# Padding three small SBUF tiles of a four-layer decoder trunk so that the large tiles start on multiples of 128 bytes

## The chip, the cores and the metric

The kernel runs on one core of one Trainium2 chip. Its metric is the device time of one execution in microseconds. Three runs of the kernel before took 856.57, 856.60 and 856.96 us, a median of 856.6. The profile is of one more execution of the same program.

## The reference

The reference passes 256 tokens of 1024 float32 features through four pre-norm residual layers, in the order A, B, C, A. Cut to what matters:

```
for i in range(4):                                  # kinds A, B, C, A
    h = rms_norm(x, norm_gain[i])
    y = mixer[i % 3](h, weights of the layer)
    x = x + y

A: u, v, z = h @ w_in            (1024 -> 3 x 2048); v = rms_norm(v)
   mixed = tril(w_s[g]) @ v + b_s            per 128-token chunk, 8 groups of 256 columns
   y = (u * mixed * silu(z)) @ w_out         (2048 -> 1024)
B: 3 groups of q, k, v with 8 heads of 128, and a gate z: h @ w_in  (1024 -> 10240)
   q, k: rms_norm with gains, rotary on the first 32 of 128 dims
   masked softmax attention per group, the groups joined by their softmax denominators
   y = (o * silu(z)) @ w_out                 (1024 -> 1024)
C: xc, z = h @ w_in              (1024 -> 2 x 2048)
   pooled = causal means of xc over windows 2, 4, 8, 16, minus xc
   y = ((pooled @ w_grp) * scale * silu(z)) @ w_out      (2048 -> 1024)
```

## The kernel before, in words

Everything is computed in float32 accuracy by products of two parts. Each operand is split into a high part (`hi_of`, L81, a ScalarE copy into the type fp32r) and a low part (`lo_of`, L84, a VectorE subtraction), and each product is three TensorE instructions that add up in PSUM: high x high, high x low, low x high (`mm3`, L75, its three lines L77 to L79). In every row of the trace the name behind `<-` stands first for the moving operand, which streams through the array column by column, and second for the stationary one, of which 128 columns are loaded before.

All projection weights come as one stream of 272 units of 512 KB. `load_units` (L127) starts their DMAs on SP's queue into 4 buffers `wr`, `split_units` makes `w…h` and `w…l` in 7 buffers each, and `next_unit` (L156) hands them out in order. A unit holds two K tiles (128 features each) of 512 columns.

The normed, transposed activations h^T lie in two tiles, `hTh` and `hTl` (L187), 8 K tiles of 256 tokens. There are three ways to use them:

- `proj_tok` (L251): 512 columns of w move, 128 tokens of h^T are stationary. Layer A has 12 such calls (v, z, u), layer B 16 (q/k and two groups' values), layer C one.
- `proj_feat` (L275): 256 tokens of h^T move, 128 columns of w are stationary. Layer B has 2 such calls (gates), layer C 7; `group` (L797) does the same with the pooled tiles `cd`, 4 times with half the K tiles.
- the third group's values in layer B (`v2p`): 256 columns of w move, h^T is stationary, 4 times.

`proj_out` (L289) multiplies each layer's y by the output weights: 512 columns of w move, the stationary operand is `y` in layers A (tag `v`), `yb` in B and `cy` in C. The last steps of it prepare the next layer's h^T. Transposes go through TensorE with the identity `ident` moving.

The other work (norms, activations, rotary, softmax, pooling) is written as generators that are resumed between pieces of the weight stream (`spawn`, `tick`, L93 to L107). Every engine keeps the order of the program as it is written out (L909 to L918).

Tiles are laid out in SBUF in the order in which their pools first meet them: first the pool `cp` (constants, x, h^T, small statistics), then `wp` (weights), then the pool of the layer. The size of each tile of a partition is rounded up to a multiple of 32 bytes, so one small tile moves the start of all that come behind it. These are the small tiles in question:

```
184  m05 = cp.tile([P, 4], F32, tag="m05", name="m05")        # exponents for the power -0.5
340  bsT = cp.tile([P, 8], F32, tag="bs", name=f"bs{layer}")   # layer A, bias of the groups
729  csc = pl.tile([P, 16], F32, name="csc")                   # layer C, scale of the channels
```

Of the kernel before, what the change touches and what calls it, by code (L numbers as in the profile page):

```python
# [48 lines left out]
def hybrid_trunk_kernel(ctx, tc, x, wts, norm_gainT, a_v_gain, a_wsT, a_bsT, b_gl, b_gv, c_scaleT,  # L49
# [7 lines left out]

    # ---------------------------------------------------------------- helpers
    def pp(name):
# [15 lines left out]
    def mm3(out_ap, lh, rh, start, stop):  # L75
        """out += l.T @ r with l and r given as (hi, lo) pairs."""
        nc.tensor.matmul(out_ap, lh[0], rh[0], start=start, stop=False, skip_group_check=True)  # L77
        nc.tensor.matmul(out_ap, lh[0], rh[1], start=False, stop=False, skip_group_check=True)  # L78
        nc.tensor.matmul(out_ap, lh[1], rh[0], start=False, stop=stop, skip_group_check=True)  # L79
# [6 lines left out]

    # ------------------------------------------------------------- interleaving
    # Work beside the stream of weight products: generators that are resumed
    # between pieces of the stream, `yield n` pieces later.
    tasks = []  # L90
# [21 lines left out]
    def need(key):  # L112
        """Go on with the tasks until one has finished `key`."""
        n = 0
        while key not in done:
            tick()
            n += 1
            assert n < 1000, (key, sorted(map(str, done)), [(e[1].__name__, e[1].gi_frame.f_lineno) for e in tasks])

    # --------------------------------------------------------- weight stream  # L120
    raws = []
# [15 lines left out]
    def split_hi(n):  # L137
        """The high parts of the first n units of the stream."""
        while split[0] < min(n, n_units):
            u = split[0]  # L140
            load_units(u + 1)
            hi, lo = pair(wp, [P, 2, HALF], "w", f"w{u}", W_BUFS)
            hi_of(hi, raws[u])
            units.append((hi, lo))
            split[0] += 1

    def split_units(n):
        """Both parts of the first n units of the stream."""
        split_hi(n)
        while lowered[0] < min(n, n_units):  # L150
            u = lowered[0]
            lo_of(units[u][1], raws[u], units[u][0])
            lowered[0] += 1
            load_units(u + 1 + RAW_BUFS)

    def next_unit():  # L156
        """The next two K tiles of 512 columns of the weight stream."""
        u = used[0]
        used[0] += 1
        split_units(u + 1)  # L160
        return units[u]

    def step(i, ahead=AHEAD):
        """After piece i of a unit: the tasks that are due, then the splitting of the weights ahead."""
        tick()
        if i % 2 == 0:
            split_hi(used[0] + ahead)
        else:
            split_units(used[0] + ahead)

    # ------------------------------------------------------------ start
    xt = [cp.tile([P, D], F32, tag=f"x{t}", name=f"x{t}") for t in range(2)]
# [10 lines left out]
    make_identity(nc, ident)  # L183
    m05 = cp.tile([P, 4], F32, tag="m05", name="m05")
    nc.gpsimd.memset(m05, -0.5)
    junk = cp.tile([P, HALF], BF16, tag="junk", name="junk")
    hTh = cp.tile([P, KT, S], F32R, tag="hTh", name="hTh")  # L187
    hTl = cp.tile([P, KT, S], F32R, tag="hTl", name="hTl")
    # the tensor engine's clock rises while it is busy
    warm = atp("warm")  # L190
# [4 lines left out]

    # ------------------------------------------------------------- norm, h^T
    def half_ss(t, n, ss):
# [16 lines left out]
    def norm_transpose(layer, t, xs):  # L214
        """h^T of a token tile: resumed between the high parts and around the low parts of the K tiles."""
        pts = []
        for n in range(2):
            pt = (trp if n else atp)(f"hp{layer}{t}{n}").rearrange("p (k c) -> p k c", c=P)
            for k in range(4):
                nc.tensor.transpose(pt[:, k], xs[:, n, k * P:(k + 1) * P], ident)  # L220
            pts.append(pt)
        sl = slice(t * P, (t + 1) * P)
        for k in range(KT):
            nc.scalar.activation(hTh[:, k, sl], pts[k // 4][:, k % 4], AF.Copy, scale=gT[:, layer, k:k + 1])  # L224
            yield k
        for k in range(KT):
            nc.vector.scalar_tensor_tensor(hTl[:, k, sl], pts[k // 4][:, k % 4], gT[:, layer, k:k + 1],  # L227
                                           hTh[:, k, sl].bitcast(F32), op0=ALU.mult, op1=ALU.subtract)
            yield KT + k
# [19 lines left out]

    # ------------------------------------------------------------ projections  # L250
    def proj_tok(name, skew=None):  # L251
        """512 columns of h @ w, token-major: two PSUM tiles. With skew the first token tile goes ahead."""
        o = [pp(f"{name}_{t}") for t in range(2)]
        if skew is not None:
            ws = [next_unit() for j in range(4)]
            for t in range(2):
                need(("h", skew, t))
                for k in range(KT):
                    w = ws[k // 2]
                    mm3(o[t], h_t(k, t), (w[0][:, k % 2], w[1][:, k % 2]), k == 0, k == KT - 1)  # L260
                    if k % 2:
                        tick()
                        if t == 1:
                            split_units(used[0] + min(k // 2 + 1, W_BUFS - 4))
            return o
        for j in range(4):
            w = next_unit()
            for kk in range(2):
                k = 2 * j + kk
                for t in range(2):  # L270
                    mm3(o[t], h_t(k, t), (w[0][:, kk], w[1][:, kk]), k == 0, k == KT - 1)
                step(kk)
        return o

    def proj_feat(name):  # L275
        """512 columns of (h @ w)^T: two PSUM tiles of two 128-feature tiles."""
        o = [pp(f"{name}_{i}") for i in range(2)]
# [11 lines left out]
    def proj_out(layer, nkt, yT):  # L289
        """x += y @ w_out, then the norm of the next layer; yT(kt, t) gives the (hi, lo) stationaries."""  # L290
        acc = [[pp(f"wo{layer}_{t}{n}") for n in range(2)] for t in range(2)]
# [41 lines left out]

    # ---------------------------------------------------------------- layer A
    def load_a(layer, j):
# [3 lines left out]
        nc.gpsimd.dma_start(wsT, a_wsT[j])  # L339
        bsT = cp.tile([P, 8], F32, tag="bs", name=f"bs{layer}")  # L340
        nc.gpsimd.dma_start(bsT, a_bsT[:, j])
        # keep j <= i (row j, columns i)
        for g in range(8):
# [4 lines left out]
    def layer_a(layer, consts, pl, mid):  # L348
# [9 lines left out]
        def v_task(n, o):  # L358
# [13 lines left out]
            if n < 3:  # L372
                return
            # rows of w_s^T scaled by the tokens' rms of v
            yield 1
# [82 lines left out]

    # ---------------------------------------------------------------- layer B
    def load_b():  # L460
# [20 lines left out]
    def layer_b(layer, consts, pl):  # L481
# [6 lines left out]
        def qk_task(hp, g, o):  # L488
# [20 lines left out]
            def rotate(t):  # L509
                """Gains and rotary on the first 32 dims."""  # L510
                ra = pl.tile([P, 4, ROPE], F32, tag="ra", name=f"ra{hp}{g}{t}", bufs=1)
# [88 lines left out]

        # (head, group, key tile) pieces of p^T; the two query tiles side by side for key tile 0
        chunks = (((0, 0, 0), (0, 1, 0)), ((0, 2, 0), (0, 0, 1), (0, 1, 1)), ((0, 2, 1), (1, 0, 0), (1, 0, 1)),
# [3 lines left out]
        def mix_task(hp, vals, szT):  # L606
# [42 lines left out]
            def gated(h):  # L649
                """(o * silu(z))^T of a head."""  # L650
                sl = slice(h * S, (h + 1) * S)
                nc.vector.tensor_tensor(szT[:, sl], o[:, sl], szT[:, sl], op=ALU.mult)
                hi_of(yh[:, h], szT[:, sl])
                yield 1
                lo_of(yl[:, h], szT[:, sl], yh[:, h])
# [34 lines left out]
        def gate(b):  # L690
            """silu(z)^T of four heads."""
            zp = proj_feat(f"bz{b}")
# [33 lines left out]

    # ---------------------------------------------------------------- layer C
    def layer_c(layer, pl):
        csc = pl.tile([P, 16], F32, name="csc")
        nc.gpsimd.dma_start(csc, c_scaleT)  # L730
# [122 lines left out]

    # ------------------------------------------------------------------ layers
    sss = [tiny(2, f"ss_{t}") for t in range(2)]
# [52 lines left out]

    # every engine keeps the order of this program  # L909
    last = {}  # L910
# [9 lines left out]

# [1 line left out]
def _units(w):  # L922
    """[K, 512] columns as [K / 256, 128, 2 * 512] units."""
    k = w.shape[0] // 256
# [120 lines left out]
```

## Time and profile before

| | |
|---|---|
| median of three runs | 856.6 us |
| profiled execution, span | 854.8 us |
| TensorE busy | 844.9 us (99%), 4600 products |
| VectorE busy | 547.4 us (64%) |
| ScalarE busy | 489.2 us (57%) |
| GpSimd busy | 55.9 us (7%) |
| weight loads on SP's queue | 272 of 512 KB, 3.9 us from issue to landing |
| mean DMA rate | 175 GB/s |

The span runs from the first to the last instruction of the profiled execution; the run's time is 1.8 us longer in the median. Products of TensorE are pipelined: a 512-column product is shown with about 0.39 us from its start to its end, but the next one starts before that end. What counts for the time is therefore the step from the start of one product to the start of the next, which is read from the first column of the timeline.

### The profile page before, as it was taken

The page shows a single profiled execution, that of the slowest core. Times are in us where ns is not written, and L with a number is a line of the kernel's source. Part 1 is how long each engine was busy: PE and PEld are TensorE (multiplying, and loading weights), DVE is VectorE, ACT ScalarE, POOL GpSimd, SP SyncE. Part 2 cuts the span into 40 slices and gives each one's busy share as a digit, 9 for nine tenths or more (in the row PEclk, how much of TensorE's full clock was granted, in tenths as well). Part 3 has the DMA queues.
Part 4 walks back from the last instruction along what each step waited for, and adds up shares of the span by engine and source line. Part 5 has one row for each costly group of instructions (what it writes and reads, how often), then busy time and mean ns, then how long its engine had stood idle before and what let it go on. Part 6 is the DMA issues. An engine that isn't in the chain of part 4 may idle for free.

```text
span 854.8 us, 12424 instructions
## 1 busy us (share of the span) xinstructions
PE 844.9 (99%) x4600; PEld 721.5 (84%) x4600; DVE 547.4 (64%) x932; ACT 489.2 (57%) x918; POOL 55.9 (7%) x79
## 2 busy tenths in 40 slices
PE   8999999999999999999999999999999999999998
PEld 6888888888988888888888889999988888888886
DVE  6766556546746667667667575797754776555551
ACT  7665444336668677677677566455443666434340
POOL 1201000000001021021021012000000000000000
PEclk9999999999999999999999999999999999999999
DMA  8756554552754345345345267447564466454541
GB/s 279 281 204 214 196 189 149 187 194 89 243 177 154 121 148 174 122 149 175 122 148 173 74 222 265 158 147 246 197 207 148 140 228 205 158 176 169 166 154 50
DMA packets 41500, 149.57 MB, mean 175 GB/s; under 512 B 4864, under 2 KB 4880, under 8 KB 41184
## 3 DMA queue, kind: packets, MB, share of 16 engines
q1 hardware_dynamic: 40320, 144.72, 50.7%
q0 software_dynamic: 976, 4.05, 1.5%
q8 instruction: 36, 0.59, 0.3%
q14 instruction: 24, 0.20, 0.1%
q10 hardware_dynamic: 144, 0.02, 0.0%
HBM read 147.72 MB, written 1.05 MB: 174 GB/s over the span
## 4 chain that ended last, share of the span: by engine, by line
PE 86%; ACT 7%; issue 2%; DVE 2%; POOL 2%; DMA 1%; SPq 0%; POOLq 0%; DVEq 0%; ACTq 0%
PE wo L77 6%; PE wo L79 6%; PE wo L78 6%; PE qk L77 4%; PE qk L78 4%; PE qk L79 4%; PE z L77 4%; PE u L77 3%; PE u L78 3%; PE u L79 3%; PE z L79 3%; PE z L78 3%; PE v L78 3%; PE v L79 3%; PE v L77 3%; ACT junk L498 2%
## 5 line engine op out<-in xcount | busy, mean ns | idle before, releaser
L503 POOL TENSOR_TENSOR qr<-qm,m 128x4 f32<-128x4 f32 x24 | 30.3, 1271 | 226.1 <-DVE qm L502 226.1
L507 ACT ACTIVATE qn<-qk,qr 128x128 f32<-128x128 f32 x96 | 27.5, 381 | 15.1 <-POOL qr L503 15.1
L498 ACT ACTIVATE junk<-qk 128x128 bf16<-128x128 f32 x96 | 26.8, 279 | 7.5 <-PE qk L79 4.9
L421 DVE TENSOR_TENSOR sz<-u,sz 128x512 f32<-128x512 f32 x16 | 11.0, 686 | 29.1 <-PE u L79 29.1
L224 ACT ACTIVATE hTh<-hp,gT 128x128 fp32r<-128x128 f32 x64 | 17.5, 382 | 16.6 <-PE hp L220 16.6
L205 POOL TENSOR_TENSOR r<-ms,m 128x1 f32<-128x1 f32 x8 | 5.4, 669 | 289.3 <-DVE ms L203 289.3
L319 DVE TENSOR_TENSOR x<-wo,x 128x512 f32<-128x512 f32 x16 | 11.0, 689 | 20.1 <-PE wo L79 20.1
L227 DVE SCALAR_TENSOR_TENSOR hTl<-hp,gT,hTh 128x128 fp32r<-128x128 f32 x64 | 18.0, 343 | 8.2 <-ACT hTh L224 8.1
L363 ACT ACTIVATE junk<-v 128x512 bf16<-128x512 f32 x16 | 9.6, 600 | 18.9 <-PE v L79 18.7
L364 DVE TENSOR_TENSOR vv<-v,kc 128x512 f32<-128x512 f32 x16 | 10.9, 688 | 13.7 <-ACT junk L363 12.8
L498 ACT ACTIVATION_READ_ACCUMULATOR junk<-qk 128x1 f32 x96 | 19.0, 198 | 0.0
L447 ACT ACTIVATE sz<-z 128x512 f32<-128x512 f32 x16 | 9.5, 598 | 16.3 <-PE z L79 15.6
L516 DVE TENSOR_TENSOR ra<-qn,kcb 128x64 f32<-128x64 f32 x48 | 10.6, 221 | 12.0 <-ACT qn L507 10.9
L528 PE MATMUL qt<-ident,qn 128*128 128x128 f32 x96 | 14.6, 274 | 2.2 <-DVE qk22l L536 0.4
L198 ACT ACTIVATE junk<-x 128x512 bf16<-128x512 f32 x16 | 10.2, 639 | 11.1 <-DVE x L319 9.5
L528 PEld LDWEIGHTS qt<-ident,qn 128*128 128x128 f32 x96 | 11.4, 141 | 6.1 <-issue 2.0
L424 DVE SCALAR_TENSOR_TENSOR yy<-mx,bs,sz 128x256 f32<-128x256 f32 x32 | 14.0, 479 | 0.6
L598 ACT ACTIVATE p<-p,rl 128x384 f32<-128x384 f32 (+1 forms) x16 | 11.5, 768 | 4.6 <-DVE rl L597 4.6
L520 DVE TENSOR_TENSOR rb<-qn,kcb 128x32 f32<-128x32 f32 x96 | 13.7, 183 | 0.0
L594 ACT ACTIVATE p<-p,nb 128x768 f32<-128x768 f32 x8 | 7.5, 938 | 8.0 <-DVE nb L593 7.9
L502 DVE TENSOR_SCALAR qm<-qs 128x4 f32<-128x4 f32 x24 | 3.3, 164 | 13.0 <-ACT junk L498 13.0
L774 ACT ACTIVATE xc<-cx 128x512 f32<-128x512 f32 x8 | 4.7, 596 | 9.7 <-PE cx L79 9.4
(2770 smaller groups left out, 3273.1 us busy)
## 6 DMA issues: line engine op xcount, KB each, us to landing
wr<-in_wts_dram SPq DMA_DIRECT2D x272, 512.0 KB, 3.9
kc<-in_a_v_gain_dram POOLq DMA_DIRECT2D x2, 1024.0 KB, 6.8
x<-in_x_dram SPq DMA_DIRECT2D x4, 256.0 KB, 4.9
kc<-in_a_wsT_dram POOLq DMA_DIRECT2D x2, 512.0 KB, 8.9
out_dram<-x SPq DMA_DIRECT2D x4, 256.0 KB, 2.0
kcb<-in_masks_dram POOLq DMA_DIRECT2D x1, 576.0 KB, 8.5
kcb<-in_b_gl_dram POOLq DMA_DIRECT2D x1, 192.0 KB, 5.9
kcb<-in_rope_dram POOLq DMA_DIRECT2D x1, 64.0 KB, 8.4
```

The lines of the kernel that those rows point to most:

```text
L77: nc.tensor.matmul(out_ap, lh[0], rh[0], start=start, stop=False, skip_group_check=True)
L78: nc.tensor.matmul(out_ap, lh[0], rh[1], start=False, stop=False, skip_group_check=True)
L79: nc.tensor.matmul(out_ap, lh[1], rh[0], start=False, stop=stop, skip_group_check=True)
L224: nc.scalar.activation(hTh[:, k, sl], pts[k // 4][:, k % 4], AF.Copy, scale=gT[:, layer, k:k + 1])
L227: nc.vector.scalar_tensor_tensor(hTl[:, k, sl], pts[k // 4][:, k % 4], gT[:, layer, k:k + 1], hTh[:, k, sl].bitcast(F32), op0=ALU.mult, op ...
L424: nc.vector.scalar_tensor_tensor(y[:, sl], mxs[n][t][:, sl], bsT[:, 2 * n + gg:2 * n + gg + 1], us[t][:, sl], op0=ALU.add, op1=ALU.mult)
L498: nc.scalar.activation(junk[:, :HD], ov[t][:, h], AF.Square, accum_out=ssq[t][:, h:h + 1])
L503: nc.gpsimd.tensor_tensor(rq[t], ms, m05, op=ALU.pow)
L507: nc.scalar.activation(qn[t][:, h], ov[t][:, h], AF.Copy, scale=rq[t][:, h:h + 1])
L520: nc.vector.tensor_tensor(rb[:, hs, s0:s0 + 16], qn[t][:, hs, s1:s1 + 16], c, op=ALU.mult)
L528: nc.tensor.transpose(pts[t][:, h], qn[t][:, h], ident)
L598: nc.scalar.activation(f, f, AF.Copy, scale=rl[i][:, 0:1])
```

## The change

The three small tiles are made larger. The parts of them that are used stay as they were: 4, 8 and 16 columns.

```
-    m05 = cp.tile([P, 4], F32, tag="m05", name="m05")
-    nc.gpsimd.memset(m05, -0.5)
+    m05_row = cp.tile([P, 32], F32, tag="m05", name="m05")
+    nc.gpsimd.memset(m05_row, -0.5)
+    m05 = m05_row[:, :4]
...
-        bsT = cp.tile([P, 8], F32, tag="bs", name=f"bs{layer}")
+        bsT = cp.tile([P, 24], F32, tag="bs", name=f"bs{layer}")[:, :8]
...
-        csc = pl.tile([P, 16], F32, name="csc")
+        csc = pl.tile([P, 32], F32, name="csc")[:, :16]
```

The rest of the diff takes out comments; the line numbers behind L185 grow by one. The order of instructions on every engine and all operands' shapes are the same in both programs; the memset has 32 columns instead of 4.

What is different is where tiles start. In both programs the address of each tile within a partition is fixed when the program is built. This table has them for the tiles that matter, as the remainder by 512 bytes. The parts of them that the products use lie at multiples of 512 bytes from the tile's start.

| tile | start mod 512, before | after |
|---|---|---|
| `x`, `ident` | 128 | 128 |
| `hTh`, `hTl` (h^T) | 160 | 256 |
| `xs` (scaled x), `kc` (constants) | 288 | 384 |
| `wr`, `w…h`, `w…l` (weights) | 96 | 256 |
| layers A and B: `v`, `y`, `wsr`, `qk`, `pT`, `yb`, `sz`, `vv` | 96 | 256 |
| layer C: `cy` | 32 | 256 |
| layer C: `cd` | 416 | 128 |

Before, all of these but `x` and `ident` start 32 bytes past a multiple of 64; after, all of them start on a multiple of 128. The statistics of a few columns stay on multiples of 32 bytes in both.

## Rows read from the trace of the kernel before

**Rows 1.** The page, part 1 (busy us, share, count) and part 4 (the chain of waits).
```profile
PE 844.9 (99%) x4600; PEld 721.5 (84%) x4600; DVE 547.4 (64%) x932; ACT 489.2 (57%) x918; POOL 55.9 (7%) x79
...
PE 86%; ACT 7%; issue 2%; DVE 2%; POOL 2%; DMA 1%; SPq 0%; POOLq 0%; DVEq 0%; ACTq 0%
```

**Rows 2.** Windows, products with the tile hTh: us, PE busy (count), granted clock, DMA share, GB/s.
```profile
0.00:854.80 854.80, 544.51 (x2016) 1.00 0.53 175
```

**Rows 3.** Timeline of TensorE, layer A, h^T stationary: start us, duration us, line, out<-moving,stationary.
```profile
699.76 0.39 PE L77 MATMUL v<-w221h,hTh 128*128 128x512 f32 x1
...
705.36 0.39 PE L77 MATMUL v<-w223h,hTh 128*128 128x512 f32 x1
```

**Rows 4.** Timeline of TensorE, output product of the first layer A.
```profile
182.71 0.39 PE L79 MATMUL wo<-w57h,y02l 128*128 128x512 f32 x1
...
188.15 0.39 PE L79 MATMUL wo<-w59h,y02l 128*128 128x512 f32 x1
```

**Rows 5.** Timeline of TensorE, output product of layer C.
```profile
639.62 0.39 PE L77 MATMUL wo<-w200h,cy1h 128*128 128x512 f32 x1
...
645.11 0.39 PE L77 MATMUL wo<-w202h,cy1h 128*128 128x512 f32 x1
```

**Rows 6.** Timeline of TensorE, layer C, h^T moving.
```profile
539.78 0.28 PE L79 MATMUL cx<-hTh,w164l 128*128 128x256 f32 x1
...
542.61 0.28 PE L79 MATMUL cx<-hTh,w165l 128*128 128x256 f32 x1
```

**Rows 7.** Timeline of TensorE, third group's values, two of four runs (22 steps each).
```profile
273.05 0.28 PE L78 MATMUL v2p<-w88l,hTh 128*128 128x256 f32 x1
...
275.64 0.28 PE L79 MATMUL v2p<-w89h,hTl 128*128 128x256 f32 x1
...
337.27 0.28 PE L78 MATMUL v2p<-w106l,hTh 128*128 128x256 f32 x1
...
339.77 0.28 PE L79 MATMUL v2p<-w107h,hTl 128*128 128x256 f32 x1
```

**Rows 8.** Timeline of TensorE, scores of one head (8 steps).
```profile
283.03 0.28 PE L77 MATMUL s<-qk00h 128*128 128x256 f32 x1
...
283.99 0.28 PE L79 MATMUL s<-qk02h,qk02l 128*128 128x256 f32 x1
```

**Rows 9.** The chain of waits in order of time: eight transposes of h^T.
```profile
198.07 0.87 PE hp L220 x8
```

**Rows 10.** Groups by line, GpSimd: two memsets (busy us, mean ns).
```profile
L773 POOL MEMSET xc<- 128x32 f32 x8 | 0.8, 135 | 44.7 <-DVE cdd L791 44.7
...
L185 POOL MEMSET m<- 128x4 f32 x1 | 0.1, 101 | 0.0
```

**Rows 11.** The chain of waits in order of time, the start: its one DMA.
```profile
3.61 7.41 DMA wr<-in_wts_dram
```

**Rows 12.** Groups by line, VectorE and ScalarE, on tiles at either kind of start.
```profile
L319 DVE TENSOR_TENSOR x<-wo,x 128x512 f32<-128x512 f32 x16 | 11.0, 689 | 20.1 <-PE wo L79 20.1
L421 DVE TENSOR_TENSOR sz<-u,sz 128x512 f32<-128x512 f32 x16 | 11.0, 686 | 29.1 <-PE u L79 29.1
...
L198 ACT ACTIVATE junk<-x 128x512 bf16<-128x512 f32 x16 | 10.2, 639 | 11.1 <-DVE x L319 9.5 <-DMA x<-in_x_dram 1.4
...
L82 ACT ACTIVATE v02h<-vv 128x512 fp32r<-128x512 f32 x2 | 1.3, 633 | 0.1
```

**Rows 13.** The chain of waits in layer B, first and last piece of one stretch off TensorE.
```profile
308.96 0.72 ACT qk10h L530 x2
...
335.67 0.88 DVE qk12l L536 x2
336.68 0.63 PE qt L528 x4
```

**Rows 14.** Windows, layer C: us, busy us of PE, PEld, DVE, ACT, POOL, clock, DMA, GB/s.
```profile
555.60:577.00 21.40, 21.40 (x185) 21.40 (x183) 20.31 (x36) 11.59 (x16) 0.25 (x2) 1.00 0.44 147
```

## The prediction

> **What bounds the kernel now.** I read the page's first and fourth parts before anything else [rows 1]. TensorE is busy for 844.9 of 854.8 us and its products are 86% of the chain of waits, so the end is set by how closely TensorE's products follow one another. The granted clock is 1.00, the upper of its two levels (2.4 GHz), over the whole span [rows 2], where 512 columns at one a cycle would take 213.3 ns and 256 columns 106.7 ns. The next view was the timeline of TensorE, for the step from one start to the next inside long runs without a wait; each pair of rows there stands 24 products apart unless I say otherwise.
>
> - 512 columns of w moving, h^T stationary: (705.36 − 699.76) / 24 = 233.3 ns [rows 3].
> - the same 512 columns of w, layer A's y stationary: 5.44 / 24 = 226.7 ns [rows 4]; layer C's y stationary: 5.49 / 24 = 228.8 ns [rows 5].
> - 256 columns of h^T moving, w stationary: 2.83 / 24 = 117.9 ns [rows 6].
> - 256 columns of w moving, h^T stationary (the third group's values): 117.7 ns in one run and 113.6 ns in another, each over 22 steps [rows 7].
> - 256 columns in the scores, both operands from the q/k tiles: 0.96 / 8 = 120.0 ns [rows 8].
> - transposes, 128 columns, limited by loading 128 stationary columns: 0.87 / 8 = 109 ns [rows 9].
>
> The reader is to see two things. First, one and the same instruction (128x512, same moving tiles) has three paces, and only the stationary tile differs, that is, where it lies. Second, the paces lie above what either stream needs alone. From the scores to layer A's output product the moving operand grows by 256 columns and the step by 106.7 ns, exactly one column a cycle: streaming alone is at full rate although its tile lies 32 bytes past a multiple of 64. Loading alone is not held up either: 109 ns is 128 columns at half the array's rate, 106.7 ns, and 2 more. The excess belongs to the stretch of each product in which the next stationary columns are read beside the moving ones. Counted so, the floor is 109 ns for 256 columns and 109 + 106.7 = 215.7 ns for 512.
>
> **The change part by part.** No instruction is added, removed or moved on any engine; SP's, ACT's and POOL's queues issue the same DMAs in the same order. One memset grows from 4 to 32 columns, from 101 ns towards the 135 ns of the 32-column memsets of layer C [rows 10], and it lies inside the 7.41 us in which the chain waits for the first weights [rows 11]: 0, and 0.03 us without that cover. The 8- and 16-column DMAs carry the same bytes. All that is left is addresses: every operand of TensorE starts on a multiple of 128 bytes instead of 32 past a multiple of 64, and the distances between moving and stationary starts change for some pairs.
>
> VectorE and ScalarE: the trace holds both kinds of tile already. x lies on a multiple of 128, sz and vv lie 32 past a multiple of 64. VectorE's sum into x takes 689 ns, its product into sz 686; ScalarE reads x in 639 ns and vv in 633 [rows 12]. Cost and gain 0, with 3 to 6 ns an instruction as the bound either way, which hides beside TensorE.
>
> Weight DMAs: they land 3.9 us after issue, against a unit that lasts 12 x 233.3 ns = 2.8 us with four loads in flight; the chain has a DMA only at the start [rows 11]. I take 0, and keep 1 us either way for the 7.41.
>
> TensorE: no row shows an aligned operand inside a dense pair of streams, so I bound it. From below: every product falls to its floor. h^T stationary: layers A have 12 products x 8 K tiles x 2 token tiles x 3 = 576 each, B 16 x 48 = 768, C 48, together 1968, each 17.6 ns better: 34.6 us. Output products: 384 in the A layers and 96 in B at 11.0 ns, 5.3 us (B's taken at A's pace); 192 in C at 13.1, 2.5 us. 256 columns with w stationary: 9 x 96 with h^T and 4 x 48 in the pooled groups (taken at the same pace), 1056 at 8.9, 9.4 us. Third group's values: 192, one run of four at 117.7 and three at 113.6, mean 114.6, 5.6 each, 1.1 us. Scores: 72 at 11, 0.8 us. (The counts are from the code; rows 2 have 2016 products with the high part of h^T, two thirds of 1968 + 864 + 192.) Sum 53.7 us. From above: each form takes its worst row, +7 us (the slower rival). Between ends so far apart I take the lower one. The excess exists only where the two streams overlap, it changes with where a tile lies, and at present every start lies in the middle of a 64-byte stretch, so that if reads go in pieces of 64 or 128 bytes nearly every piece takes in two of them. That pieces have this size is my assumption; no row shows it.
>
> What comes back of the 53.7: layer B has four stretches in which the chain runs over ScalarE, VectorE and GpSimd from the q/k products to the transposes, the second from 308.96 to 336.68 us [rows 13]; three of 27.7 us and a first one of 15.1 us make 98 us, 11.5% of the span, and a faster TensorE only waits there: 6.2 us. In layer C VectorE is busy for 20.31 of 21.40 us [rows 14]; 7.5% less is 19.8 us: 0.5 us. So 53.7 − 6.7 = 47.0, the span goes from 854.8 to 807.8, and with the 1.8 us by which the median of 856.6 stands above the profiled span, 810 us.
>
> The Trainium skill (SBUF — State Buffer, Door 1, the note on cachelines) has 16-byte lines and a penalty for each crossing into a new line. Every start was a multiple of 32 already and stays one, so by that rule the step stays 233.3 ns and the sum is 0: it is the second rival's rule. The skill (TensorE: Matmul & The Clock Gate, Step-by-step) also says that loading the next weights takes no read bandwidth from the running product; by it 512 columns would have one pace whatever lies stationary, and 233.3 against 226.7 ns [rows 3, 4] disagree.
>
> **The rivals.**
>
> Only the distance counts. Layer A's y starts at the same phase of 512 bytes as w (both 96) and runs at 226.7; h^T is 64 bytes off and runs at 233.3; layer C's y is 64 off the other way. Afterwards all but the pooled tiles are at distance 0. Then h^T goes to 226.7: 1968 x 6.6 = 13.0 us; C's output 192 x 2.1 = 0.4; against it the 256-column products go to the scores' 120.0, also distance 0: 864 x 2.1 = 1.8 and 192 x 5.4 = 1.0. Net 10.6, less 11.5%: 9.4 us, 847 us. For it: it explains the order of the 512-column paces. Against it: 64 off is the slowest pace at 512 columns and the fastest at 256, and rows 7 show two paces at one distance.
>
> Nothing changes: pieces of 32 bytes or less, or an excess that belongs to this data type, or padding that does not reach the operands. 856.6 us. For it: streaming and loading alone are at full rate without alignment. Against it: the three paces of one instruction.
>
> Slower: one common phase is the bad one. With every tile on a multiple of 128, the moving stream, the stationary load and the other engines' accesses start in the same place of every 128 bytes and meet there. The price is that each form goes to its worst row: A's and B's output products from 226.7 to 233.3, 480 x 6.6 = 3.2 us; C's, 192 x 4.5 = 0.9; 256 columns to 120.0, 1056 x 2.1 = 2.2 and 192 x 5.4 = 1.0. Sum 7.3, so 864 us. It decides as soon as h^T's products do not fall below 233 ns. For it: the scores, both operands at one phase, are the slowest 256-column form. Against it: the output products at one phase are the fastest 512-column form.
>
> **How the numbers follow.** Aligned pairs read freely: 0.45, 810 us, its own range 802 (nothing comes back) to 833 (half the excess stays). Distance only: 0.22, 847. Nothing: 0.14. Slower: 0.17, around 864. Something between: 0.02, a small gain. Faster by over 0.2% (1.7 us, what a measurement of this kernel can tell) is 0.45 + 0.22 + 0.02 = 0.69, within it 0.14, slower 0.17. The range goes from 800 to 861: it leaves out most of the slower case and a remainder below.
>
> **What would show it.** In the changed profile the steps of the six forms above are read again. Right: 512 columns near 216 ns whatever is stationary, 256 columns near 109, VectorE's and ScalarE's means unchanged, TensorE's waits in layer B's four stretches longer. 226.7 and 120 ns everywhere speak for the distance alone, 233.3 and 117.9 unchanged for no effect, 233 beside 120 for the slower case. The forecast is wrong if h^T's step stays above 230 ns.

## The result and the profile after

The changed kernel takes 850.8 us in the median of four runs (850.58 to 850.96); the kernel before took 856.8 beside it (856.57 to 857.22). The ratio is 0.9931, with a 95% interval of 0.9919 to 0.9942: 6.0 us faster, where 47 were forecast. The profiled execution has a span of 849.1 us (before 854.8), so the two traces account for 5.7 of it.

With the runs for the experiments the kernel before shows that it has two times of its own: of all 45 runs of it, on several chips, 18 took 852.4 to 853.4 us and 27 took 856.2 to 857.3. All four that stand beside the change took the upper one, so the 6.0 us are against that; against the lower one the change is worth some 2 us. What the two times come from is followed up below.

The page's parts 1 and 4 of the kernel after answer to [rows 1]:

```profile
PE 837.2 (99%) x4600; PEld 724.6 (85%) x4600; DVE 546.8 (64%) x932; ACT 488.9 (58%) x918; POOL 57.4 (7%) x79
...
PE 86%; ACT 7%; DVE 2%; issue 2%; POOL 2%; DMA 1%; SPq 0%; POOLq 0%; DVEq 0%
```

Nothing has changed places: TensorE still sets the end. The products with `hTh`, over the whole span (us, PE busy, PEld, DVE, ACT, each with its count, then clock, DMA share, GB/s), as in [rows 2]:

```profile
0.00:849.10 849.10, 540.85 (x2016) 351.55 (x2016) 17.94 (x64) 17.49 (x64) 1.00 0.53 176
```

The granted clock is 1.00 again, so every difference in a step is one of cycles. The timeline of TensorE after (start us, duration us, line, out<-moving,stationary), two products that lie 24 steps apart for each form: h^T stationary as in [rows 3], layer A's y as in [rows 4], layer C's `cy` as in [rows 5], h^T moving as in [rows 6].

```profile
698.98 0.39 PE L77 MATMUL v<-w222h,hTh 128*128 128x512 f32 x1
...
704.42 0.39 PE L77 MATMUL z<-w224h,hTh 128*128 128x512 f32 x1
...
177.75 0.39 PE L79 MATMUL wo<-w57h,y02l 128*128 128x512 f32 x1
...
183.19 0.39 PE L79 MATMUL wo<-w59h,y02l 128*128 128x512 f32 x1
...
640.05 0.39 PE L77 MATMUL wo<-w201h,cy1h 128*128 128x512 f32 x1
...
645.49 0.39 PE L77 MATMUL wo<-w203h,cy1h 128*128 128x512 f32 x1
...
535.91 0.28 PE L77 MATMUL cx<-hTh,w164h 128*128 128x256 f32 x1
...
538.79 0.28 PE L77 MATMUL cx<-hTh,w165h 128*128 128x256 f32 x1
```

The first three pairs are 5.44 us apart, 226.7 ns a product: the 512-column forms have one pace now. h^T fell from 233.3, `cy` from 228.8, and y, which had 226.7 before, stayed. The last pair is 2.88 us apart: 120.0 ns, where it was 117.9. The third group's values, 22 steps apart as in [rows 7]:

```profile
333.70 0.28 PE L78 MATMUL v2p<-w106l,hTh 128*128 128x256 f32 x1
...
336.34 0.28 PE L79 MATMUL v2p<-w107h,hTl 128*128 128x256 f32 x1
```

2.64 / 22 = 120.0 ns, against 117.7 and 113.6. So the 256-column forms with h^T became slower. By stage (starts of the same product in both traces, us from the span's start):

| stage, between starts of | before | after | change |
|---|---|---|---|
| first layer A, to the first q/k product | 200.16 | 197.23 | −2.9 |
| layer B, to layer C's first product | 302.76 | 302.25 | −0.5 |
| layer C, to the last layer A's first product | 159.57 | 160.51 | +0.9 |
| last layer A, to the end | 192.3 | 189.1 | −3.2 |

Layer B got next to nothing. The stretch that answers to [rows 13] starts after the change with this piece of the chain of waits (start us, us, what):

```profile
305.39 0.72 ACT qk10h L531 x2
```

It ends with the transposes `qt`, here from the timeline of TensorE, before and after; the bracket is the time for which TensorE waited just ahead of them, and for what:

```profile
336.68 0.63 PE L528 MATMUL qt<-ident,qn 128*128 128x128 f32 x4 [0.38 <-DVE qk12l L536]
...
333.12 0.63 PE L529 MATMUL qt<-ident,qn 128*128 128x128 f32 x4 [0.55 <-DVE qk12l L537]
```

The stretch lasts 333.12 − 305.39 = 27.73 us, before 336.68 − 308.96 = 27.72. From these transposes to the same ones of the next group of heads it is 64.07 us after (333.12 to 397.19) and 64.11 before (336.68 to 400.79), although 192 products of 512 columns with h^T stationary lie between, 1.3 us at 6.6 ns each. Added up from the starts in both traces, these products save only 0.74 us: in runs of six between other work they gain almost nothing (the `qk` run from 351.37 us takes 1.48 us, after the change, from 347.92, 1.47). The 48 products of `v2p` take 0.26 us more, and two waits for VectorE ahead of transposes grow by 0.41 together: the one in the rows above from 0.38 to 0.55, another from 0.25 to 0.49.

VectorE, groups by line, as in [rows 12]:

```profile
L422 DVE TENSOR_TENSOR sz<-u,sz 128x512 f32<-128x512 f32 x16 | 11.0, 686 | 28.0 <-PE u L79 28.0
```

`sz` moved from 32 past a multiple of 64 to a multiple of 128 and its product takes 686 ns as before. In layer C, from 551.5 to 572.9 us as in [rows 14], VectorE's 36 instructions take 20.31 us as before, while TensorE gets through 181 products in place of 185.

### The profile page after: what moved, and what is told of

The parts are those of the page before. It is cut to its first block, busy times and chain, and to the rows that moved or that the text cites. A ratio compares the mean times of both kernels' runs of the same rounds, so it can differ in the third digit from the quotient of the medians.

```text
span 849.1 us, 12424 instructions
## 1 busy us (share of the span) xinstructions
PE 837.2 (99%) x4600; PEld 724.6 (85%) x4600; DVE 546.8 (64%) x932; ACT 488.9 (58%) x918; POOL 57.4 (7%) x79
## 4 chain that ended last, share of the span: by engine, by line
PE 86%; ACT 7%; DVE 2%; issue 2%; POOL 2%; DMA 1%; SPq 0%; POOLq 0%; DVEq 0%
PE wo L77 6%; PE wo L79 6%; PE wo L78 6%; PE qk L77 4%; PE qk L78 4%; PE qk L79 4%; PE z L77 3%; PE z L79 3%; PE z L78 3%; PE u L77 3%; PE u L78 3%; PE u L79 3%; PE v L78 3%; PE v L79 3%; PE v L77 3%; ACT junk L499 2%
## 5 line engine op out<-in xcount | busy, mean ns | idle before, releaser
L364 ACT ACTIVATE junk<-v 128x512 bf16<-128x512 f32 x16 | 9.6, 600 | 17.6 <-PE v L79 17.5
L517 DVE TENSOR_TENSOR ra<-qn,kcb 128x64 f32<-128x64 f32 x48 | 10.6, 221 | 12.0 <-ACT qn L508 10.9
L599 ACT ACTIVATE p<-p,rl 128x384 f32<-128x384 f32 (+1 forms) x16 | 11.5, 769 | 4.7 <-DVE rl L598 4.7
L345 POOL TENSOR_SCALAR_AFFINE_SELECT kc<-kc 128x128 f32<-128x128 f32 x16 | 9.8, 649 | 14.4 <-DMA kc<-in_a_wsT_dram 8.6
```

Source lines behind the costliest of these rows:

```text
L599: nc.scalar.activation(f, f, AF.Copy, scale=rl[i][:, 0:1])
```

## The experiments

The theory of the prediction, from here on "alignment": the step falls when the starts lie on multiples of 64 or 128. Its rival, "distance": what counts is how far the stationary start lies behind the moving one, modulo some power of two, wherever both lie.

**The step by itself.** Products without any other work, 24 in a row with the same operands; `n` is the number of moving columns, `d` the distance in bytes from the moving to the stationary start, `a` a common shift of both at distance 0, `b` a common shift with bf16 operands. It leaves out the whole layer computation.

```
+    def run(name, n, moff, soff, m=mov, s=sta, rep=REP):
+        o = ps.tile([P, 512], F32, tag="o", name=name, bufs=4)
+        for i in range(rep):
+            nc.tensor.matmul(o[:, :n], s[:, soff:soff + P], m[:, moff:moff + n], start=i == 0, stop=i == rep - 1,
+                             skip_group_check=True)
```

> This kernel leaves out the whole model: it copies x to the output and runs nothing but groups of 24 TensorE products on two tiles, one moving and one stationary, both at the same phase of 512 bytes (names: n = columns, d = bytes by which the stationary start is ahead of the moving start, a = bytes by which both are shifted together, b = the same distance with bf16 operands). Theory 1, the distance alone counts: at 512 columns 226.7 ns a step at d0, 233.3 at d64 and about 229 at d448; at 256 columns 120 at d0 and 113.6 or 117.7 at d64; all a groups at 226.7 and 120 like d0, whatever the shift. Theory 2, the start's multiple counts: d0 at 226.7 and 120, and the a4, a8, a16, a32 and a96 groups slower than d0 by 6 ns or more while a64 is like d0; d64 and d128 as fast as d0. Neither theory says how the other distances lie; the lowest of them bounds what a better layout can give. For bf16 the floor worked out before (109 and 215.7 ns) would be reached if the excess comes from 4-byte columns.

The timeline of TensorE; one row is a group of 24, and the step is the difference of two neighbouring starts over 24:

```profile
18.67 5.60 PE L35 MATMUL n512d0x<-mov,sta 128*128 128x512 f32 x24
24.11 5.61 PE L35 MATMUL n512d16x<-mov,sta 128*128 128x512 f32 x24
...
40.75 5.76 PE L35 MATMUL n512d64x<-mov,sta 128*128 128x512 f32 x24
46.34 5.72 PE L35 MATMUL n512d80x<-mov,sta 128*128 128x512 f32 x24
...
85.43 5.66 PE L35 MATMUL n512d192x<-mov,sta 128*128 128x512 f32 x24
90.92 5.76 PE L35 MATMUL n512d208x<-mov,sta 128*128 128x512 f32 x24
...
107.58 5.60 PE L35 MATMUL n512d256x<-mov,sta 128*128 128x512 f32 x24
113.02 5.76 PE L35 MATMUL n512d320x<-mov,sta 128*128 128x512 f32 x24
...
135.15 3.03 PE L35 MATMUL n256d0x<-mov,sta 128*128 128x256 f32 x24
138.02 3.01 PE L35 MATMUL n256d16x<-mov,sta 128*128 128x256 f32 x24
...
146.53 2.89 PE L35 MATMUL n256d64x<-mov,sta 128*128 128x256 f32 x24
149.25 3.01 PE L35 MATMUL n256d80x<-mov,sta 128*128 128x256 f32 x24
...
169.23 2.99 PE L35 MATMUL n256d192x<-mov,sta 128*128 128x256 f32 x24
172.06 2.96 PE L35 MATMUL n256d208x<-mov,sta 128*128 128x256 f32 x24
...
211.54 5.65 PE L35 MATMUL n512a32x<-mov,sta 128*128 128x512 f32 x24
217.03 5.64 PE L35 MATMUL n512a64x<-mov,sta 128*128 128x512 f32 x24
222.51 5.63 PE L35 MATMUL n512a96x<-mov,sta 128*128 128x512 f32 x24
...
250.43 5.34 PE L35 MATMUL n512b32x<-mob,stb 128*128 128x512 bf16 x24
255.61 5.34 PE L35 MATMUL n512b64x<-mob,stb 128*128 128x512 bf16 x24
```

| distance, bytes | 512 columns, ns | 256 columns, ns | pair of the kernel before |
|---|---|---|---|
| 0 | 226.7 | 119.6 | y stationary; scores |
| 64 | 232.9 | 113.3 | h^T stationary; `v2p` |
| 192 | 228.8 | 117.9 | `cy` stationary; h^T and `cd` moving |

The distance alone gives back every pace of the kernel before to within 0.4 ns (233.3, 226.7, 228.8, 117.9, 120.0, and 113.6 for three runs of `v2p` out of four). At 256 bytes the 512-column step is 5.44 / 24 = 226.7 ns again, at 512 bytes 227.1, and at 320 the 232.9 of distance 64: the period is 256 bytes. At 256 columns one group does not fit: distance 320 has 2.83 / 24 = 117.9 ns, where 64 has 113.3. The repeats further below take that up.

Alignment does little from 32 bytes on: a common shift of 32 bytes gives 5.49 / 24 = 228.8 ns, one of 64 bytes 5.48 / 24 = 228.3, one of 96 bytes 227.9, all within 2.1 ns of the unshifted pair, and the multiple of 64 no better than its neighbours. Smaller shifts do cost something, against the distance theory: 237.5 ns at 4 bytes, 231.3 at 8, 230.0 at 16. The alignment theory wanted a shift of 32 or 96 bytes to cost 6 ns or more, and distance 64 to be as fast as 0; neither is so.

The 215.7 ns of the prediction belong to another type: bf16 steps by 5.18 / 24 = 215.8 ns at shifts of 32 and 64 alike. The Trainium skill (TensorE: Matmul & The Clock Gate, Back-to-back issue gap) gives N / 2.4 + 2.5 ns as the gap of an isolated product and names no type; by it 512 columns would take an estimated 215.8 ns. This trace agrees for bf16 and not for the 4-byte type, which takes 226.7 at its best.

**The bias tile alone.** Only layer A's small tile is padded, so that h^T and the weights have distance 0 while all large tiles stay 32 bytes past a multiple of 64.

```
-        bsT = cp.tile([P, 8], F32, tag="bs", name=f"bs{layer}")
+        bsT = cp.tile([P, 24], F32, tag="bs", name=f"bs{layer}")[:, :8]
```

> One part of the change alone: only the bias tile is padded, by 64 bytes. h^T keeps its start (160 mod 512), the weights move from 96 to 160, A's and B's y with them; every large tile still lies 32 bytes past a multiple of 64, layer C's pair keeps its distances. Theory 1 (distance): h^T stationary 226.8 ns, h^T moving 119.9, C's output products still 228.8; 851 us, like the whole change within 1 us. Theory 2 (multiple of 64 or 128): nothing is aligned, so 233.3 and 117.9 as before and 856.8 us.

850.85 us (850.42 to 851.39, ten runs), 0.9956 [0.9940, 0.9971] of the kernel before on the same chip, where that took both its times. The last layer A, h^T stationary, 24 steps:

```profile
698.78 0.39 PE L77 MATMUL v<-w222h,hTh 128*128 128x512 f32 x1
...
704.22 0.39 PE L77 MATMUL z<-w224h,hTh 128*128 128x512 f32 x1
```

5.44 us, 226.7 ns: the step of the changed kernel, and its time too (850.8 us), with all large tiles still 32 bytes past a multiple of 64.

**The exponent tile alone.** All large tiles go to multiples of 64, and every distance stays what it was.

```
-    m05 = cp.tile([P, 4], F32, tag="m05", name="m05")
+    m05_row = cp.tile([P, 32], F32, tag="m05", name="m05")
```

> Another part alone: only the tile of -0.5 is padded, by 96 bytes. Every large tile moves by 96 and so starts on a multiple of 64, and all distances stay as they were before (h^T 64 ahead of the weights, C's y 64 behind). Theory 1 (distance): 233.3 and 117.9 ns, 856.8 us, no change. Theory 2 (multiple of 64): the gain of the whole change, 851 us or less; if only multiples of 128 count, part of it.

853.05 us (852.75 to 853.41, twelve runs), 0.9976 [0.9961, 0.9991]. h^T stationary in layer A, and h^T moving in layer C:

```profile
697.04 0.39 PE L77 MATMUL v<-w221h,hTh 128*128 128x512 f32 x1
...
702.64 0.39 PE L77 MATMUL v<-w223h,hTh 128*128 128x512 f32 x1
...
535.33 0.28 PE L77 MATMUL cx<-hTh,w163h 128*128 128x256 f32 x1
...
538.05 0.28 PE L77 MATMUL cx<-hTh,w164h 128*128 128x256 f32 x1
```

5.60 / 24 = 233.3 ns, as before: aligned tiles alone gain h^T nothing. But layer C runs at 2.72 / 24 = 113.3 ns in place of 117.9, at the same distance of 192. Neither theory has this. 864 products (672 with h^T, 192 with `cd`) by 4.4 ns are 3.8 us, and the two times of the kernel before lie 3.7 us apart: the guess was that one distance has two steps at 256 columns. One thing the guess leaves open: all twelve runs here lie at the lower time, where the kernel before has 18 of 45. So where the tiles lie seems to bear on which step is taken, and an effect of alignment on that is not ruled out.

**Aligned, but far.** The kernel after with a larger bias tile: all large tiles on multiples of 128, h^T at distance 128 from the weights.

```
-        bsT = cp.tile([P, 24], F32, tag="bs", name=f"bs{layer}")[:, :8]
+        bsT = cp.tile([P, 56], F32, tag="bs", name=f"bs{layer}")[:, :8]
```

> The changed kernel with the bias tile padded by 128 bytes more: all large tiles still start on multiples of 128, but the weights, y and layer C's y move by 128 against h^T. Theory 1 (distance, period 256 bytes as e1 showed): h^T stationary at distance 128 goes back to 233.3 ns a step, 256-column products stay at about 120, output products stay at 226.7; the 7 us that h^T's products gained go, so 858 us, above the kernel before. Theory 2 (multiples of 128 bytes count): 226.8 ns, 850.8 us as the changed kernel.

856.89 us (856.40 to 857.47, twelve runs), 1.0019 [1.0005, 1.0033] of the kernel before, which took both its times beside it; the upper one alone has a median of 856.5. The gain is gone, with everything aligned as the change wants it.

```profile
701.77 0.40 PE L77 MATMUL v<-w221h,hTh 128*128 128x512 f32 x1
...
707.36 0.39 PE L77 MATMUL v<-w223h,hTh 128*128 128x512 f32 x1
```

5.59 / 24 = 232.9 ns for h^T stationary, and 2.85 / 24 = 118.8 ns for h^T moving in layer C (534.76 to 537.61 us). Alignment is out as the cause of the gain at 512 columns.

**Each form at its own distance.** The kernel after, where layer C alone has h^T and `cd` shifted so that the stationary w lies at distance 64 from the moving start (modulo 256); elsewhere the distance is 0.

```
-    hTh = cp.tile([P, KT, S], F32R, tag="hTh", name="hTh")
-    hTl = cp.tile([P, KT, S], F32R, tag="hTl", name="hTl")
+    hT_all = [cp.tile([P, KT * S + 64], F32R, tag=f"hT{c}", name=f"hT{c}") for c in "hl"]
+    hT_at = [[h[:, o:o + KT * S].rearrange("p (k s) -> p k s", s=S) for h in hT_all]
+             for o in (0, 0, 48, 0)]
...
-            dh, dl = pair(pl, [P, 4, S], "cd", f"cd{g}", 2)
+            dh, dl = [c[:, 16:16 + 4 * S].rearrange("p (k s) -> p k s", s=S)
+                      for c in pair(pl, [P, 4 * S + 64], "cd", f"cd{g}", 2)]
```

> The changed kernel with h^T of layer C and the pooled tiles cd placed so that the stationary weights start 64 bytes ahead of the moving operand (mod 256); everything else keeps distance 0. Theory 1 with the curve of e1: 256-column products of layer C go from 119.9 and 118.7 to 113.3 ns, 672 x 6.6 + 192 x 5.4 = 5.5 us; the 48 products of layer C with h^T stationary go from 226.8 to 228.8 or 229.6, 0.1 us the other way; layer C is paced by TensorE, so 845.5 us. If VectorE holds layer C (20.3 of 21.4 us busy in one window) less than half of it shows: above 848. Theory 2: the pooled tiles and h^T are on multiples of 64 but not of 128 here, so no gain or a loss: 850.8 us or more.

848.95, 848.65, 845.59, 849.13, 845.95 and 849.15 us, median 848.8, 0.9917 [0.989, 0.9944] of the kernel before: the best version here, and again one with two times. The profiled run was one of the slower, with 117.8 ns in layer C; the two faster ones are near the 845.5 that were expected. Above 848, where the other four lie, was expected if VectorE holds layer C back; the two profiles at the end of this section decide that against VectorE.

**Fewer stationary columns.** The bench again, with 32 to 128 stationary columns (`c`), and 256 columns at distance 192 and at 64, each eight times over after 3 to 10 other products (`r0` to `r7`, 48 products each).

```
-            nc.tensor.matmul(o[:, :n], s[:, soff:soff + P], m[:, moff:moff + n], ...
+            nc.tensor.matmul(o[:cols, :n], sta[:, d // 4:d // 4 + cols], mov[:, :n], ...
```

> Again only groups of products, without the model (names: n = moving columns, d = distance in bytes, c = stationary columns; r0 to r7 are repeats of one form, 48 products each, after 3 to 10 products of another form). Theory A, that of the prediction's floor: the excess over one column a cycle comes from reading the next stationary columns beside the moving ones; with 32 stationary columns instead of 128 it falls to a quarter, from 226.7 to about 216 to 218 ns at d0 and from 233.3 to about 219 at d128. Theory B: 226.7 and 113.3 ns are the rate of this data type, 17 cycles for 16 columns, whatever is loaded beside it; then 226.7 stays at c32 for every distance, and only what lies above it falls. On the repeats: at distance 192 a 256-column stream falls into either of two steps, 117.7 or 113.3 ns, and keeps it, so the eight repeats show both; at distance 64 all are 113.3.

```profile
42.05 5.71 PE L35 MATMUL n512d64c32x<-mov,sta 128*32 128x512 f32 x24
47.60 5.75 PE L35 MATMUL n512d64c64x<-mov,sta 128*64 128x512 f32 x24
...
86.37 2.89 PE L35 MATMUL n256d0c32x<-mov,sta 128*32 128x256 f32 x24
89.09 2.88 PE L35 MATMUL n256d0c64x<-mov,sta 128*64 128x256 f32 x24
...
133.70 5.82 PE L35 MATMUL n256d192r2x<-mov,sta 128*128 128x256 f32 x48
139.35 1.56 PE L35 MATMUL pre3x<-mov,sta 128*128 128x512 f32 x6
140.76 5.60 PE L35 MATMUL n256d192r3x<-mov,sta 128*128 128x256 f32 x48
146.20 1.77 PE L35 MATMUL pre4x<-mov,sta 128*128 128x512 f32 x7
...
182.74 5.67 PE L35 MATMUL n256d64r1x<-mov,sta 128*128 128x256 f32 x48
...
188.75 5.87 PE L35 MATMUL n256d64r2x<-mov,sta 128*128 128x256 f32 x48
```

With a quarter of the weights to load, 512 columns step by 5.55 / 24 = 231.3 ns at distance 64, and by 231.7 and 230.8 at 0 and 128. That fits neither expectation: the prediction's floor wanted 216 to 219, the other theory 226.7. The lowest of all twelve 512-column forms is 226.7, and the lowest of the 256-column forms 2.72 / 24 = 113.3. These are 544 and 272 cycles at 2.4 GHz, 17 for every 16 columns, and no 512- or 256-column product with 4-byte operands steps faster over a run of 24 anywhere here. At 256 columns what lies above does go with the load: at distance 0 the step is 119.6 ns with 128 stationary columns and 113.3 with 32, and with 32 it is 113.3 at all three distances.

The rows `r2` and `r3` at distance 192 are one and the same form, and the row behind each shows where it ends: 5.65 / 48 = 117.7 ns in the one, 5.44 / 48 = 113.3 in the other. Two steps at one distance are shown on TensorE alone (from 119 to 227 us of this run no other engine is busy, and the DMA share is 0.00); seven repeats of the eight at distance 192 had the slower one. At distance 64 all eight were expected at 113.3, but two of them are slower as well: the last two rows show 5.67 us for one repeat and 5.87 for the next, 0.20 / 48 = 4.2 ns a product.

**The two times, in the kernels.** The kernel before and the one with each form at its own distance were profiled twice more, unchanged.

> The kernel before once more. Its own runs have taken either 852.4 to 853.4 or 856.2 to 857.3 us. Two steps at one distance: where the run takes about 853 us, the long stretch of layer C with h^T moving has a step of 113.3 ns and the time from the product cz2 to wo2 is 98.9 us; where it takes about 856.7, 117.8 ns and 102.6 us; the 512-column steps are 233.3 ns with h^T stationary and 229 with cy either way. Rival, the difference lies elsewhere (waits for weights, layer B, the clock): layer C is alike in both, at 117.8 ns and 102.6 us, and a run at 853 us is shorter at another place.

> The same program again: 853 us with 113.3 ns and 98.9 us in layer C, or 856.7 with 117.8 ns and 102.6 us by the two steps; by the rival layer C has 117.8 ns and 102.6 us at either time.

> The kernel whose layer C has the stationary w 64 bytes ahead of the moving operand, again. Two steps: 845.8 us with 113.3 ns for h^T and cd moving in layer C, or 849.0 us with 117.8; h^T stationary 226.7 to 227.7 ns in both. Rival, the difference lies elsewhere: 117.8 ns at either time.

> The same program again: 845.8 us with 113.3 ns in layer C, or 849.0 with 117.8; by the rival 117.8 ns at either time.

The kernel before took 856.41 and 856.33 us, both its upper time, at 117.8 ns in layer C in both profiles; its lower time was not caught. The other took 845.51 and 849.32. Layer C, h^T moving, 24 steps, of the first and then of the second:

```profile
534.83 0.28 PE L77 MATMUL cx<-hTh,w164h 128*128 128x256 f32 x1
...
537.55 0.28 PE L77 MATMUL cx<-hTh,w165h 128*128 128x256 f32 x1
```

```profile
535.02 0.28 PE L77 MATMUL cx<-hTh,w164h 128*128 128x256 f32 x1
...
537.85 0.28 PE L77 MATMUL cx<-hTh,w165h 128*128 128x256 f32 x1
```

2.72 / 24 = 113.3 and 2.83 / 24 = 117.9 ns, the same program on the same chip. The step holds from the start of layer C's long run, behind its last transposes, to its end (some 516.5 us to 610.3 and to 614.1). From the second z call to the output product layer C takes 98.9 and 102.5 us: 3.6 of the 3.8 us between the two runs, and the other 0.2 lie ahead of it. At 113.3 ns the time is the expected one, so VectorE does not hold layer C back.

The slower execution did not have the slower step from the beginning. Ahead of layer C's two groups of transposes, 18 steps apart:

```profile
512.12 0.28 PE L78 MATMUL cz<-hTl,w156h 128*128 128x256 f32 x1
...
514.16 0.28 PE L78 MATMUL cz<-hTl,w156h 128*128 128x256 f32 x1
```

2.04 / 18 = 113.3 ns, and behind the transposes 117.9. In the faster execution the twelve products between the two groups of transposes step by 117.5 ns (514.95 to 515.89, 8 steps) and those ahead and behind by 113.3. So in these two, but for the first half dozen products behind a 512-column run (116 to 123 ns in both), the step changes only where transposes break the run.

For the kernel before the same cause is likely, by the size (3.7 us) and by the run with the exponent tile alone, but not shown in a profile of it.

## Why the prediction was wrong

**The bound, and what costs nothing:** right. TensorE's step sets the time, the memset, the DMAs, VectorE (686 ns for `sz` in both) and ScalarE (633 ns before and 632 after for `v02h` from `vv`) moved nothing that shows. The stretch of layer B off TensorE kept its 27.7 us, as forecast.

**The floor of TensorE's step:** this is the step that failed. The prediction said that the excess of a product "belongs to the stretch of each product in which the next stationary columns are read beside the moving ones", and "Counted so, the floor is 109 ns for 256 columns and 109 + 106.7 = 215.7 ns for 512". The 106.7, "exactly one column a cycle", was 226.7 less 120.0. But 226.7 is the best step at 512 columns, and 120.0 a poor one at 256, whose best is 113.3: two forms at different places above their floors were subtracted. Best from best it is 113.4 ns for 256 columns, 17 cycles for 16, and no run went below that, with a quarter of the weights either. A product with h^T in a long run gained 233.3 − 226.7 = 6.6 ns, not 17.6 (the largest term of the sum, 34.6 us), and y nothing (forecast 11.0 ns). No distance in the bench gives more. A bf16 product has the floor that was forecast. The sign of failure that the prediction named, h^T's step above 230 ns, did not come either: the step fell to 226.7 and the forecast was wrong all the same.

**The choice between the ends:** wrong by the same thought. It rested on pieces of 64 or 128 bytes, which no row showed; the tiles at 32 past a multiple of 64 run at 226.7 ns once the distance is 0, and aligned ones run at 232.9 at distance 128. The Trainium skill (SBUF — State Buffer, Door 1) has 16-byte lines and a penalty for crossing into a new one. That starts on multiples of 32 bytes gain nothing from more alignment, as the prediction drew from it, agrees with this; that the time would then not change does not, since the rule says nothing of distances.

**The sign for 256 columns:** wrong. They were to fall by 8.9 ns and rose by 2.1; layer C's long run from its second z call to the output product takes 104.28 us for 102.64.

**The rival that only the distance counts** had the mechanism and the paces: 226.7 for all 512-column products, 120.0 for h^T moving and for `v2p`. It was given 0.22, because the two paces of `v2p` at one distance [rows 7] seemed to speak against it. The likely reading is that they were the two steps of one distance, seen in the first profile and put down as a contradiction. Its sum of 9.4 us was too high as well. Before anything comes back it had 10.6 us: 7.6 in the two layers A, 3.6 in B, −0.7 in C (from its own terms, but for rounding). The stages measured 6.1, 0.5 and −0.9, together 5.7. The 6.6 ns hold in long runs only. In layer A a run of twelve between transposes gains 0.02 us (2.88 to 2.86, from 735.15 us before and 730.72 after), where 12 x 6.6 ns are 0.08. In layer B the share of the four stretches off TensorE, 11.5% of the span, was the wrong measure: short runs gain nothing there, `v2p` loses, and the two waits grow, so that none of the 64 us rounds gets shorter.

**Layer C's return** was also reckoned too small, by the prediction's own rule: its 0.5 us are for one window of 21.4 us, and layer C's long run lasts 102.64, which makes some 2.4. It did not come to matter, since layer C became slower.

**What stays open:** why the step depends on the distance with a period of 256 bytes and in opposite order for 512 and 256 columns, why 512 columns with 32 stationary ones step by 231 ns, and what decides which of two steps a run of products takes. Here only the fact, its size and its lasting through a run are shown.

## What to carry to other kernels

Before a floor is worked out from two forms, each is to be measured at its own best: a bench of the bare instruction over all operand distances takes one execution, and would have shown 226.7 and 113.3 here. With 4-byte operands, place the stationary tile by its distance from the moving one modulo 256 bytes, form by form: 0 for 512 columns, and for 256 columns 64, which can still fall into the slower step of 117.8 ns but not to 120. Don't trade a 512-column gain for a 256-column loss. Where one form shows two paces in one trace, take the program for one with two times, and compare many runs of it before a change of under 1% is believed.

## What the runs showed of the hardware

- TensorE with 4-byte operands: never under 226.7 ns for 512 moving columns and 113.3 for 256 at the granted clock of 1.00, at 32 to 128 stationary columns; bf16 takes 215.8.
- The step depends on the distance of the two starts, at 512 columns with a period of 256 bytes: 226.7 to 234 ns at 512 columns, 113.3 to 120 at 256. In bf16 no common shift made a difference; its distance was not varied.
- The 256-column step at distances 192 and 64 has two values (113.3 and 117.8), taken by a run of products and kept for up to 98 us; in a whole kernel that is 3.6 us between two executions of one program.
- At 512 columns fewer stationary columns are not faster: at distance 0 they take 5.56 / 24 = 231.7 ns with 32 and 226.7 with 128. At 256 columns they are: 113.3 with 32 and 119.6 with 128.
